# A mixture of experts on one core: gathered rows instead of one-hot products, weight tiles of 8 KB rows, four accumulators open at once

## The chip, the core and the metric

The kernel runs on one of the eight cores of a Trainium2 chip. The core has TensorE (PE in the profile, with its weight loads shown apart as PEld), VectorE (DVE), ScalarE (ACT), GpSimd (POOL) and SyncE (SP), which here only issues transfers; 16 DMA engines move data between DRAM and the on-chip memory SBUF, and PE writes into the accumulator memory PSUM. The metric is the time of one execution in microseconds of the device, the median of several runs.

## What is computed

Three model blocks follow each other on 512 tokens of 1024 features. The first two (an mLSTM and attention block, then a recurrent and gating block) and the mixers of the third are not touched. The third block ends in a mixture of 32 experts, four for each token, and a gated embedding. The reference, cut to that part and written in short:

```
logits = x @ router_w + router_b                     # [512, 32]
top4, idx = top_k(logits, 4);  gates = softmax(top4)
for expert e, for each token that chose e:
    h        = x_tok @ w_gate_up[e] + b_gate_up[e]   # [1024] @ [1024, 2048]
    gate, up = min(h[:1024], 7), clip(h[1024:], -7, 7)
    act      = (up + 1) * gate * sigmoid(1.702 * gate)
    y_tok   += gates[tok, e] * (act @ w_down[e] + b_down[e])
z = layer_norm(alpha * x + y);  out = layer_norm(alpha * z + sigmoid(z @ ple_gate_w + b) * (p @ ple_proj))
```

Each expert has 2 x 4 MB of gate and up weights and 4 MB of down weights, all float32.

## The kernel before

**Two-part products.** A float32 product is made of three passes in the format float32r: each operand is split into a high part and a low remainder (`hi`, `lo`), and `mm3` issues high by high, low by high and high by low (lines 165 to 167). A block of weights of 1 MB lands in a tile `wl` by a transfer that SP issues (line 92); ACT writes its high part `wh` (line 97) and DVE the remainder `wo` (line 98). `ring` hands out the tiles: in the experts' stage five `wl`, three `wh`, three `wo`.

**Routing.** `deepnorm` normalises token tile by token tile and calls `Moe.route`, which writes the rows to DRAM (`x3d`), chooses the experts, and leaves in `pos1` each token's slot in its experts (line 1454); it also splits x into the two parts `xs` (lines 109 and 110). An expert's first 96 tokens (`CAP`) are handled here; `crowded` takes any further ones in a branch after the end. Experts go in groups of three (`GRP`).

**Picking.** `mark` writes `hot`, which is 1 where a token has a slot (line 1507), for a group. `picked` multiplies x by it: four products of 128 x 288 over the four token tiles (line 1516) give 128 features of the slots of three experts, and one copy (line 1517 or 1550) keeps them. A group takes 64 such products. Those of the next group are spread over the experts of this one. `places` (four small products, line 1495) reads token number, gate and destination row of each slot.

**An expert.** `up` runs once for each half of the hidden columns: for the gate columns and then for the up columns it adds the bias by a product over 64 rows (line 1617: rows of the two parts of all experts' biases, picked by the column `sel` of the expert), and adds two weight blocks of 512 x 512 taken as four feature tiles. So one accumulator `pgu` is finished before the next is begun. `glu` reads them (lines 1535 to 1539), `turn` transposes the result (line 1525) and splits it into `h`. `down` takes four blocks of 512 x 512 for two accumulators `pd`, ACT scales them by the gate into `y` (line 1639), and POOL adds the rows to `yd` in DRAM by an indirect transfer (line 1722). In program order an expert is: first half of up, down of the expert before, second half of up; the compiler's scheduler interleaves the instructions of neighbouring calls on each engine, and each engine then runs its list in order.

**Accumulators.** PSUM's eight banks are shared as four `gemm` (for `pgu` and `pd`), three `aux` and one `hold`.

**The end.** `ple` reads `yd` back, normalises, and makes the last products; its gate biases are products over 64 rows too (line 1795).

Of the kernel before, what the change touches and what calls it, by code (L numbers as in the profile page):

```python
# [11 lines left out]
F32 = mybir.dt.float32  # L12
# [7 lines left out]
P = 128  # L20
S = 512
D = 1024
# [9 lines left out]
class Env:  # L32
    BANKS = {"gemm": 4, "aux": 3, "hold": 1}

    def __init__(self, ctx, tc):
        self.tc, self.nc = tc, tc.nc
        nc = self.nc
        self.cst = ctx.enter_context(tc.tile_pool(name="cst", bufs=1))
# [3 lines left out]
        self.psp = ctx.enter_context(tc.tile_pool(name="ps", bufs=4, space=bass.MemoryType.PSUM))  # L42
# [5 lines left out]
        self.n = 0  # L48
# [30 lines left out]

    def ps(self, s, tag="aux"):  # L80
# [19 lines left out]

    def wblock(self, w, k0, nk, c0, n, *more, **opts):
# [3 lines left out]
    def split(self, hi, lo, src, scale=None):  # L105
        """src * scale into two float32r parts."""
# [8 lines left out]
    def bank(self, ctx, n):  # L115
        """n tiles [128, 4, 512] on the right until ctx closes."""
# [20 lines left out]
    def give(self, *tiles):  # L137
        """What was read for the last time."""
# [6 lines left out]
    def lend(self, n):  # L145
        """n more tiles each for the two parts of weights; returns what ends that."""
# [12 lines left out]
    def acts(self, k, bank=None):  # L159
        """Tiles for a feature-major operand of k feature tiles: k/4 pairs [128, 4, 512]."""  # L160
# [8 lines left out]
    def gemm_tok(self, xs, K, w, c0, cn, consume, eng=None):  # L169
        """Token-major: consume(tt, col, n, psum) for psum[tok, col:col+n] = x @ w[:, col:col+n]."""  # L170
# [52 lines left out]
    def bcast(self, pool, src, n, tag):  # L223
        """A row of n values in DRAM onto all partitions."""
# [4 lines left out]
    def transpose_in(self, xs, t, src, k=KT):  # L229
        """src [tok of tile t, k*128 features] into the feature-major pairs xs."""  # L230
# [8 lines left out]
    def rstd(self, pool, ssq, n, eps, tag):  # L239
        """(ssq / n + eps) ** -0.5 of a few columns."""  # L240
# [8 lines left out]
    def rms(self, pool, x, gain, eps, out, scratch=None):  # L249
        """out = x * rsqrt(mean(x^2) + eps) * gain of one token tile [128, 1024]."""  # L250
# [6 lines left out]
    def layer_norm(self, pool, x, eps, out, gain, bias, tag=""):  # L257
        """out = (x - mean) * rstd * gain + bias of one token tile [128, 1024]."""
# [17 lines left out]
def block1(e, a, res, more):  # L276
    """The first block's x, and what the second's first product takes."""
# [17 lines left out]
    with ExitStack() as ph:  # L295
# [8 lines left out]
        # -------- i_k, i_w, m_i, m_f in one stationary block  # L304
# [33 lines left out]
        # index keys: norm over the 64 features, on both partition halves  # L338
# [24 lines left out]
        # relative bias: strips of 256 keys per head, less the value of far keys  # L363
# [23 lines left out]
        # causal mask inside one tile of 128 keys: 0 where key <= query  # L387
# [11 lines left out]
        # -------- mLSTM gates, a head per partition  # L399
# [37 lines left out]
        # selectors of a head's row: pairs of 64 partitions, and all 128  # L437
# [9 lines left out]
        # token-major columns of c, the key weights and the floor of the denominator  # L447
# [11 lines left out]
        # 0 where key <= query within one chunk of 64, keys on partitions  # L459
# [1408 lines left out]
```

## Time and profile before

| what | value |
|---|---|
| time, median of 3 runs | 3298.0 us (3294.18 to 3298.59) |
| profiled execution, first to last instruction | 3294.7 us |
| busy share of that span | PE 98%, PEld 74%, DVE 65%, ACT 47%, POOL 8% |
| DMA over the span | 626.96 MB, mean 190 GB/s |
| experts' stage, first bias product to last scatter | 1939.35 to 3208.18 us |

A busy share is an average over stages with different limits. What an edit in the experts' stage is worth has to be read from that stage alone, which is 39% of the span. PE's records overlap (a product's modelled end lies after the start of the next), so the spacing of the starts is what tells its pace.

### The profile page before, as it was taken

How to read it: one execution, taken by the hardware profiler on the slowest of the kernel's cores; microseconds unless marked ns; L12 is line 12 of the kernel's file. 1: busy time of each engine (PE TensorE's matmuls, PEld its weight loads, DVE VectorE, ACT ScalarE, POOL GpSimd, SP SyncE). 2: the span in 40 equal slices, each digit the busy share in tenths (PEclk: the TensorE clock that was granted, in tenths of full speed). 3: DMA queues.
4: the chain of work that ended last, by engine and by line, in shares of the span. 5: the costliest groups of instructions: out<-in, count | busy, mean ns of one | idle time of the engine just before them, and what ended most of it. 6: DMA issues, size and time to landing. Idle time of an engine off the chain costs nothing. (4 is left out here: it accounts for less than half of the span.)

```text
span 3294.7 us, 37481 instructions
## 1 busy us (share of the span) xinstructions
PE 3222.8 (98%) x15051; PEld 2434.6 (74%) x15051; DVE 2128.5 (65%) x2381; ACT 1564.5 (47%) x1655; POOL 272.7 (8%) x203
## 2 busy tenths in 40 slices
PE   7999999999999999999999999999999999999997
PEld 6776877878777788788778776666666666666665
DVE  5854687444636523822335778788888788888786
ACT  5343333323625223222322347777677667766662
POOL 2310011101000000200000100000000000000001
PEclk9997999999999999999999999999999999999999
DMA  4211465333222333232232259999999999999992
GB/s 143 77 39 62 147 218 201 115 109 97 64 64 64 89 113 122 87 109 92 83 119 90 91 204 330 332 324 319 330 329 329 327 327 325 323 331 325 328 328 104
DMA packets 324081, 626.96 MB, mean 190 GB/s; under 512 B 25144, under 2 KB 32672, under 8 KB 323834
## 3 DMA queue, kind: packets, MB, share of 16 engines
q1 hardware_dynamic: 320314, 611.89, 54.2%
q0 software_dynamic: 3584, 12.58, 1.9%
q8 instruction: 120, 1.97, 0.2%
q14 instruction: 63, 0.52, 0.0%
HBM read 603.43 MB, written 21.01 MB: 190 GB/s over the span
## 5 line engine op out<-in xcount | busy, mean ns | idle before, releaser
L98 DVE TENSOR_TENSOR wo<-wl,wh 128x2048 fp32r<-128x2048 f32 (+2 forms) x531 | 1190.3, 2254 | 627.8 <-ACT wh L97 625.8
L97 ACT ACTIVATE wh<-wl 128x2048 fp32r<-128x2048 f32 (+2 forms) x537 | 1009.0, 1885 | 744.6 <-PE pf L167 319.1
L165 PE MATMUL pf<-ah,wh 128*128 128x512 f32 (+1 forms) x1520 | 563.4, 371 | 0.6 <-ACT wh L97 0.6
L166 PE MATMUL pf<-ah,wo 128*128 128x512 f32 (+1 forms) x1520 | 562.2, 370 | 1.2 <-DVE wo L98 1.2
L167 PE MATMUL pf<-al,wh 128*128 128x512 f32 (+1 forms) x1520 | 561.5, 370 | 0.0
L165 PEld LDWEIGHTS pf<-ah,wh 128*128 128x128 f32 x1520 | 287.4, 189 | 56.4 <-ACT cy L727 6.9
L166 PEld LDWEIGHTS pf<-ah,wo 128*128 128x128 f32 x1520 | 287.0, 189 | 51.4 <-DVE wo L98 1.4
L167 PEld LDWEIGHTS pf<-al,wh 128*128 128x128 f32 x1520 | 286.5, 189 | 51.7 <-issue 3.7
L165 PE MATMUL pgu<-wh,xe 128*96 128x512 f32 x784 | 316.7, 404 | 0.0
L167 PE MATMUL pgu<-wo,xe 128*96 128x512 f32 x784 | 310.1, 396 | 1.8 <-DVE wo L98 1.7
L166 PE MATMUL pgu<-wh,xe 128*96 128x512 f32 x784 | 310.3, 396 | 0.0
L166 PE MATMUL pd<-wh,h 128*96 128x512 f32 x512 | 201.9, 394 | 0.0
L165 PE MATMUL pd<-wh,h 128*96 128x512 f32 x512 | 201.9, 394 | 0.0
L167 PE MATMUL pd<-wo,h 128*96 128x512 f32 x512 | 201.5, 393 | 0.1
L1722 POOL DMA_INDIRECT yd<-y,dst x32 | 79.1, 2472 | 1212.1 <-ACT y L1639 1112.1
L165 PEld LDWEIGHTS pgu<-wh,xe 128*96 128x96 f32 x784 | 126.3, 161 | 69.3 <-issue 22.2
L167 PEld LDWEIGHTS pgu<-wo,xe 128*96 128x96 f32 x784 | 126.6, 161 | 57.6 <-DVE wo L98 6.0
L166 PEld LDWEIGHTS pgu<-wh,xe 128*96 128x96 f32 x784 | 126.7, 162 | 45.9
L165 PE MATMUL pa<-wh,ah 128*128 128x512 f32 x352 | 143.0, 406 | 0.0
L167 PE MATMUL pa<-wo,ah 128*128 128x512 f32 x352 | 141.5, 402 | 0.2 <-DVE wo L98 0.2
L166 PE MATMUL pa<-wh,al 128*128 128x512 f32 x352 | 141.7, 402 | 0.0
L165 PE MATMUL pdn<-wh,ah 128*128 128x512 f32 x352 | 139.1, 396 | 0.7 <-ACT wh L97 0.7
(484 smaller groups left out, 4615.2 us busy)
## 6 DMA issues: line engine op xcount, KB each, us to landing
wl<-w_gate_up SPq DMA_DIRECT2D x256, 1024.0 KB
wl<-w_down SPq DMA_DIRECT2D x138, 1024.0 KB
wl<-w_in SPq DMA_DIRECT2D x54, 1024.0 KB
wl<-w_ada SPq DMA_DIRECT2D x24, 1024.0 KB
wl<-w_up SPq DMA_DIRECT2D x20, 1024.0 KB
wl<-w_ffn_in SPq DMA_DIRECT2D x20, 1024.0 KB
wl<-w_out SPq DMA_DIRECT2D x12, 1024.0 KB
wl<-w_ffn_out SPq DMA_DIRECT2D x10, 1024.0 KB
```

Source lines behind the costliest of these rows:

```text
L97: nc.scalar.activation(hi[:, :nk, :n], land[:, :nk, :n], AF.Copy)
L98: (eng or nc.vector).tensor_tensor(lo[:, :nk, :n], land[:, :nk, :n], hi[:, :nk, :n].bitcast(F32), op=ALU.subtract)
L165: mm(out, st[0], mv[0], start=first, stop=False)
L166: mm(out, st[1], mv[0], start=False, stop=False)
L167: mm(out, st[0], mv[1], start=False, stop=last)
L1722: self.e.nc.gpsimd.indirect_dma_start(out=self.yd, out_offset=bass.IndirectOffsetOnAxis(ap=dst[:, :1], axis=0), in_=y, in_offset=None, com ...
```

## The change

- The rows of an expert's tokens are gathered from `x3d` by an indirect transfer on POOL into `xg`, and transposed and split by `turn`, the helper that `h` goes through; `picked`, `share` and the split of x into `xs` are gone. In place of `xs`, `wh` and `wo` get two more tiles each (`lend`), so they have five.
- Weights come in through `wtile`: each transfer is 128 rows of 8 KB (a feature tile of all 2048 gate and up columns, or two neighbouring rows of `w_down` per partition) instead of 512 rows of 2 KB. `turn` gets `step=2` for `h`, which takes every second column, to suit the pairs of rows.
- `up` runs once for an expert, with its four accumulators open: all four biases first, then feature tile by feature tile. `glu` follows for both halves. `down` takes its two accumulators from `hold`; PSUM is laid out anew as four `gemm`, two `aux` and two `hold`.
- The bias products take all 128 rows (`sel` is 0 in the rows that don't belong), here and in `ple`.
- In an expert's program order the gather of the expert after next, and the two transposes of the next one's rows, stand between the feature tiles of `up`.

```diff
+    def wtile(self, src, **opts):
+        return self.weights(lambda land: [(land.rearrange("p a b -> p (a b)"), src)], 4, 512, **opts)
...
-    def picked(self, hot, f, part, out, copy, tag):
-        pt = e.ps("pt", tag)[:, :GRP * CAP]
-        for t in range(NT):
-            x = self.xs[part][t // 2].rearrange("p (h a) n -> p h (a n)", h=2)[:, t % 2, f * P:(f + 1) * P]
-            nc.tensor.matmul(pt, x, hot[:, t].rearrange("p e s -> p (e s)"), start=t == 0, stop=t == NT - 1)
-        copy(out, pt)
...
         for j in range(4):
-            nc.tensor.transpose(pt[:, j, :], src[:, j * P:(j + 1) * P], e.ident[:w, :w])
+            c = j // step * step * P
+            nc.tensor.transpose(pt[:, j, :], src[:, c:c + step * P].rearrange("p (f i) -> p i f", i=step)[:, j % step, :],
+                                e.ident[:w, :w])
...
+        e.layout(gemm=4, aux=2, hold=2)
+        back = e.lend(2)
...
+        def fetch(i):
+            pi, *took[i] = self.places(hots[p][:, :, j, :], self.tge[:, :, i, :])
+            src = wp.tile([P, 1], I32, tag="src", name=e.name("src"))[:CAP, :]
+            nc.vector.tensor_copy(src, pi[:, 0:1])
+            rows[i] = mp.tile([P, D], F32, tag="xg", name=e.name("xg"))[:CAP, :]
+            nc.gpsimd.indirect_dma_start(out=rows[i], out_offset=None, in_=self.xd,
+                                         in_offset=bass.IndirectOffsetOnAxis(ap=src[:, :1], axis=0))
...
+            if i < N_EXP:
+                side = {2: lambda: fetch(i + 2), 4: lambda: turn_x(i + 1, 0), 6: lambda: turn_x(i + 1, 1)}
+                gs = self.up(i, [xs.pop((i, g)) for g in range(2)], side)
             if i:
+                self.down(i - 1, hs, *took.pop(i - 1))
+            if i < N_EXP:
+                hs = [self.turn(g, entry("h", 2), 1.0 / SW, 2) for g in gs]
...
-    def up(self, i, xs, f):
+    def up(self, i, xs, side):
-        for c in (f * 512, D + f * 512):
-            p = e.ps("pgu", "gemm")[:CAP, :]
-            nc.tensor.matmul(p, self.sel[:2 * N_EXP, i:i + 1].to_broadcast([2 * N_EXP, CAP]), self.bgu[:2 * N_EXP, c:c + 512],
+        acc = [e.ps("pgu", "gemm")[:CAP, :] for _ in range(4)]
+        for c in range(4):
+            nc.tensor.matmul(acc[c], self.sel[:, i:i + 1].to_broadcast([P, CAP]), self.bgu[:, c * 512:(c + 1) * 512],
                              start=True, stop=False)
+        for k in range(KT):
+            hi, lo = e.wtile(w[k * P:(k + 1) * P, :], hold=self.pos1[:, 0, NT - 1:] if i == 0 and k > 1 else None)
+            for c in (0, 2, 1, 3):
+                e.mm3(acc[c], (xh[:, k % 4, :], xl[:, k % 4, :]), (hi[:, c, :], lo[:, c, :]), False, k == KT - 1)
+        return [self.glu(acc[f], acc[2 + f]) for f in range(2)]
...
-        acc = [e.ps("pd", "gemm")[:CAP, :] for _ in range(2)]
+        acc = [e.ps("pd", "hold")[:CAP, :] for _ in range(2)]
+        for j in range(4):
+            hi, lo = e.wtile(w[j * 256:(j + 1) * 256, :].rearrange("(p i) n -> p (i n)", i=2))
```

The scheduler's lists show three places where the change moves instructions. First DVE, in the middle of the stage, where it reads an expert's accumulators. Before, from one expert (`pgu` is an accumulator, `wo` a remainder of weights, L98 the split, L1535 to L1539 `glu`, L113 the split of `h`):

```order
L98 TENSOR_TENSOR wo_17463<-wl_17460,wh_17462 128x2048
L1538 TENSOR_SCALAR u_17455<-pgu_17414 96x512
L1539 SCALAR_TENSOR_TENSOR g_17452<-u_17455,g_17452 96x512
L98 TENSOR_TENSOR wo_17481<-wl_17478,wh_17480 128x2048
L98 TENSOR_TENSOR wo_17501<-wl_17498,wh_17500 128x2048
L1535 TENSOR_SCALAR g_17534<-pgu_17458 96x512
L113 SCALAR_TENSOR_TENSOR h_17540<-pt_17541,h_17540 128x384
L98 TENSOR_TENSOR wo_17519<-wl_17516,wh_17518 128x2048
```

Now, at the end of one expert's `up` (L103 is the split, L122 the split of `h`):

```order
L103 TENSOR_TENSOR wo_14197<-wl_14194,wh_14196 128x2048
L1535 TENSOR_SCALAR g_14212<-pgu_14027 96x512
L1538 TENSOR_SCALAR u_14215<-pgu_14029 96x512
L1535 TENSOR_SCALAR g_14218<-pgu_14028 96x512
L1539 SCALAR_TENSOR_TENSOR g_14212<-u_14215,g_14212 96x512
L1538 TENSOR_SCALAR u_14221<-pgu_14030 96x512
L103 TENSOR_TENSOR wo_14347<-wl_14344,wh_14346 128x2048
L1539 SCALAR_TENSOR_TENSOR g_14218<-u_14221,g_14218 96x512
L103 TENSOR_TENSOR wo_14365<-wl_14362,wh_14364 128x2048
L122 SCALAR_TENSOR_TENSOR h_14302<-pt_14303,h_14302 128x384
```

The reads of the four accumulators, which stood one or two at a time between splits of weights, now stand together, with a split among them.

Second, PE between the end of an `up` and the transposes of its result. Before, the rows just ahead of such transposes (L165 to L167 are `mm3`, L1525 the transposes of `turn`, `g_15424` the result of `glu`); fourteen products of `down`, of which three stand here, have been issued since the last of the accumulator that `g_15424` waits for:

```order
L167 MATMUL pd_15439<-wo_15444,h_15216 96x512
L165 MATMUL pd_15440<-wh_15461,h_15216 96x512
L166 MATMUL pd_15440<-wh_15461,h_15216 96x512
L1525 MATMUL pt_15517<-ident,g_15424 128x96 x4
L1516 MATMUL pt_15524<-spot,xs_12602 128x288 x2
L1516 MATMUL pt_15524<-spot,xs_12603 128x288 x2
```

Now (L174 to L176 are `mm3`, L1605 the bias, L1524 the transposes; `g_14790` and `g_14796` are the results of the `up` that has just ended with `pgu_14610`):

```order
L175 MATMUL pgu_14610<-wh_14774,xe_14475 96x512
L176 MATMUL pgu_14610<-wo_14775,xe_14475 96x512
L174 MATMUL pd_14803<-wh_14807,h_14591 96x512
L175 MATMUL pd_14803<-wh_14807,h_14591 96x512
L174 MATMUL pd_14804<-wh_14807,h_14591 96x512
L175 MATMUL pd_14804<-wh_14807,h_14591 96x512
L1605 MATMUL pgu_14896<-bgu,sel 96x512
L1605 MATMUL pgu_14897<-bgu,sel 96x512
L1605 MATMUL pgu_14898<-bgu,sel 96x512
L1605 MATMUL pgu_14899<-bgu,sel 96x512
L1524 MATMUL pt_14881<-ident,g_14790 128x96 x4
L1524 MATMUL pt_14889<-ident,g_14796 128x96 x4
```

Only four products of `down` and four biases stand between the end of `up` and the transposes of its result. Over the 32 experts the place of the first transpose repeats with a period of five: behind 8, 10, 48, 17 and 10 products.

Third, PE at the start of the stage. Before (L1436 is the last token tile's routing, L1452 and L1453 the counts for `pos1`, L1516 the picks, `hot` the marks):

```order
L1516 MATMUL pt_13146<-hot_13142,xs_12600 128x288
L1436 MATMUL pl_13089<-rw,xt_13076 128x32 x8
L1452 MATMUL pp_13109<-mask,ones 128x32 x3
L1516 MATMUL pt_13146<-hot_13142,xs_12600 128x288
L1516 MATMUL pt_13146<-hot_13142,xs_12601 128x288
L1516 MATMUL pt_13152<-hot_13142,xs_12602 128x288 x2
L1516 MATMUL pt_13152<-hot_13142,xs_12603 128x288
L1516 MATMUL pt_13158<-hot_13142,xs_12600 128x288 x2
L1516 MATMUL pt_13158<-hot_13142,xs_12601 128x288
L1516 MATMUL pt_13164<-hot_13142,xs_12602 128x288 x2
L1516 MATMUL pt_13164<-hot_13142,xs_12603 128x288
L1453 MATMUL pp_13109<-mask,upper 128x32
```

Now (L1501 is `places`, L1733 and L1740 are `biased`, L1488 `routed`, L1524 the transposes of gathered rows `xg`):

```order
L1501 MATMUL pi_13142<-tge,hot_13140 96x4 x3
L1733 MATMUL pg_13157<-ident,four_13158 128x128
L1501 MATMUL pi_13142<-tge,hot_13140 96x4
L1740 MATMUL pb_13164<-bgu,gs_13161 128x512 x2
L1740 MATMUL pb_13168<-bgu,gs_13161 128x512 x2
L1733 MATMUL pg_13173<-ident,four_13174 128x128
L1740 MATMUL pb_13180<-bgu,gs_13177 128x512 x2
L1740 MATMUL pb_13184<-bgu,gs_13177 128x512 x2
L1501 MATMUL pi_13189<-tge,hot_13140 96x4 x4
L1488 MATMUL pn_13204<-mask,ones 128x32 x4
L1524 MATMUL pt_13215<-ident,xg_13155 128x96 x4
```

The picks are gone from between the routing; the first expert now waits for a gather, and the work of `biased`, `places` and `routed`, which stood behind the first expert's products, stands ahead of them.

## Rows read from the trace of the kernel before

**Rows 1.** The page's parts 1 and 2: busy time, and 40 slices of the span.

```profile
PE 3222.8 (98%) x15051; PEld 2434.6 (74%) x15051; DVE 2128.5 (65%) x2381; ACT 1564.5 (47%) x1655; POOL 272.7 (8%) x203
...
PE   7999999999999999999999999999999999999997
```

**Rows 2.** Window of three experts: us, busy PE, PEld, DVE, ACT, POOL, clock, DMA, GB/s.

```profile
2512.62:2631.92 119.30, 118.93 (x546) 82.36 (x545) 97.82 (x71) 83.24 (x70) 7.63 (x4) 1.00 0.95 326
```

**Rows 3.** Waits from 2100 to 3200 us: total, times, longest, all in us.

```profile
ACT wh L97 <- PE pgu L166: 91.1, 91, 1.8
...
DVE g L1535 <- PE pgu L167: 68.6, 51, 2.1
DVE wo L98 <- ACT wh L97: 62.8, 100, 2.2
```

**Rows 4.** Timeline of PE around a bias: start us, duration us.

```profile
2519.29 0.39 PE L167 MATMUL pgu<-wo,xe 128*96 128x512 f32 x1
2519.61 0.47 PE L1617 MATMUL pgu<-bgu,sel 64*96 64x512 f32 x1
2520.01 0.48 PE L165 MATMUL pgu<-wh,xe 128*96 128x512 f32 x1
2520.33 0.39 PE L166 MATMUL pgu<-wh,xe 128*96 128x512 f32 x1
```

**Rows 5.** Timeline of PE where one accumulator group follows another.

```profile
2498.18 0.39 PE L167 MATMUL pgu<-wo,xe 128*96 128x512 f32 x1
2498.41 0.40 PE L165 MATMUL pd<-wh,h 128*96 128x512 f32 x1
```

**Rows 6.** Timeline of PE around transposes and picks.

```profile
2501.65 0.49 PE L1525 MATMUL pt<-ident,g 96*128 96x96 f32 x4
2501.93 0.77 PE L1516 MATMUL pt<-spot,xs 128*128 128x288 f32 x4
...
2510.95 1.75 PE L1516 MATMUL pt<-spot,xs 128*128 128x288 f32 x12
2512.62 0.47 PE L1617 MATMUL pgu<-bgu,sel 64*96 64x512 f32 x1
```

**Rows 7.** Line 1516 over the whole trace: ns min/median/max, first and last start.

```profile
L1516 PE MATMUL pt<-spot,xs x640: 289/294/404, 1962.1 to 3110.9; 128*128 128x288 f32 x160
```

**Rows 8.** Groups by form, 2512.62 to 2631.92 us: busy us, mean ns.

```profile
L98 DVE TENSOR_TENSOR wo<-wl,wh 128x2048 fp32r<-128x2048 f32 x37 | 83.9, 2285 | 7.1 <-ACT wh L97 7.0
...
L1535 DVE TENSOR_SCALAR g<-pgu 96x512 f32<-96x512 f32 x6 | 4.1, 687 | 8.2 <-PE pgu L167 8.2
...
L113 DVE SCALAR_TENSOR_TENSOR h<-pt,h 128x384 fp32r<-128x384 f32 x6 | 3.3, 547 | 0.0
...
L1507 DVE TENSOR_TENSOR spot<-slot,pos 128x1152 fp32r<-128x1152 f32 x1 | 1.3, 1345 | 0.0
```

**Rows 9.** DMA, 3172 to 3190 us: GB/s in 40 slices, then packets and total.

```profile
GB/s 373 400 387 378 391 369 410 396 382 405 396 382 401 400 378 391 396 382 387 391 291 382 419 387 405 423 246 118 414 391 414 410 391 260 191 332 246 410 419 319
DMA packets 3315, 6.60 MB, mean 367 GB/s; under 512 B 96, under 2 KB 96, under 8 KB 3314
```

**Rows 10.** DMA over 0 to 12 us, where 4 KB rows of x land: GB/s.

```profile
GB/s 0 0 0 0 0 0 137 177 328 328 314 396 287 259 259 232 273 314 287 314 423 382 423 437 437 396 423 437 410 437 383 195 106 171 188 91 42 22 8 17
```

**Rows 11.** DMA from 1706 to 1714 us, where the 8 KB rows of the biases land.

```profile
GB/s 0 0 0 0 0 0 0 0 0 0 0 0 0 0 0 0 0 0 0 0 0 0 205 246 205 205 205 246 0 123 287 369 266 287 0 328 369 184 266 174
```

**Rows 12.** DMA issues, 2512.62 to 2631.92 us: median us from issue to landing.

```profile
yd<-y,dst POOLq DMA_INDIRECT x4, 9.1
```

**Rows 13.** Timeline of PE and DVE at the start of the stage.

```profile
1919.27 1.97 PE L1432 MATMUL pt<-ident,xres 128*128 128x128 f32 x8 [4.33 <-DVE xres L269]
...
1926.47 0.36 DVE L1448 TENSOR_REDUCE mask<-hot 128x32 f32<-128x128 f32 x1
...
1929.51 0.22 DVE L1454 SCALAR_TENSOR_TENSOR pos<-pp,mask 128x32 f32<-128x32 f32 x1 [2.22 <-PE pp L1453]
...
1939.75 0.47 PE L165 MATMUL pgu<-wh,xe 128*96 128x512 f32 x1
```

More of the change, by code (lines that the diff above doesn't have):

```diff
@@ L1483, in routed @@
         nc.vector.tensor_copy(self.count[:, E:], most)
-    def share(self):
-        self.xs = [[self.e.slot("xs", F32R, 0) for _ in range(NT // 2)] for _ in range(2)]
     def places(self, hot, tge):
@@ L1547, in run @@
         e, nc, wp = self.e, self.e.nc, self.wp
-        groups = -(-N_EXP // GRP)
-        took, hots, parts = {}, {}, {}
-        copies = lambda o, i: nc.scalar.activation(o, i, AF.Copy), nc.vector.tensor_copy
-        def entry(nm):
-            return wp.tile([P, 2, 4, GRP * CAP], F32R, tag="xe", name=e.name(nm), bufs=3)
-        def mark(p, hot, *cuts):
-            hots[p] = hot
-            for t0, t1 in zip((0, *cuts), (*cuts, NT)):
-                self.chosen(hot[:, t0:t1], self.pos1[:, GRP * p:GRP * (p + 1), t0:t1])
@@ L1560, in pick @@
-        def pick(p, j, n, start=False):
-            every = [(g, k, part) for g in range(2) for k in range(4) for part in range(2)]
-            m = len(every)
-            for x, (g, k, part) in enumerate(every[j * m // n:(j + 1) * m // n]):
-                if not k and not part:
-                    both = self.spot[:, :8 * GRP * CAP].rearrange("p (a k n) -> p a k n", a=2, k=4) if g and p % 2 else entry("xe")
-                    for i in range(GRP):
-                        parts[GRP * p + i, g] = both, slice(i * CAP, (i + 1) * CAP)
-                both = parts[GRP * p, g][0]
-                self.picked(hots[p], 4 * g + k, part, both[:, part, k, :], copies[part if start else 0],
-                            ("hold", "gemm", "gemm", "gemm", "gemm")[x % 5] if start else "aux")
@@ new lines, in entry, with turn_x @@
+        def entry(nm, n):
+            return mp.tile([P, 2, 4, CAP], F32R, tag=nm, name=e.name(nm), bufs=n)
+        def turn_x(i, g):
+            if i < N_EXP:
+                xs[i, g] = self.turn(rows[i][:, g * 512:(g + 1) * 512], entry("xe", 3))
+        mark(0)
+        fetch(0)
+        self.biased(NT - 2)
+        self.biased(NT - 1)
+        fetch(1)
+        self.routed()
+        for g in range(2):
+            turn_x(0, g)
+        hs = None
+        for i in range(N_EXP + 1):
+            if i < N_EXP:
+                side = {2: lambda: fetch(i + 2), 4: lambda: turn_x(i + 1, 0), 6: lambda: turn_x(i + 1, 1)}
+                gs = self.up(i, [xs.pop((i, g)) for g in range(2)], side)
+            if i:
+                self.down(i - 1, hs, *took.pop(i - 1))
+            if i < N_EXP:
+                hs = [self.turn(g, entry("h", 2), 1.0 / SW, 2) for g in gs]
@@ L1618, in up @@
                              start=True, stop=False)
-            for k0 in (0, 4):
-                hi, lo = e.wblock(w, k0, 4, c, 512, hold=None if i or f or c == 0 and k0 == 0 else self.pos1[:, 0, NT - 1:])
-                xh, xl = xs[k0 // 4]
-                for k in range(4):
-                    e.mm3(p, (xh[:, k, :], xl[:, k, :]), (hi[:, k, :], lo[:, k, :]), False, k0 + k == 7)
-            acc.append(p)
-        return self.glu(*acc)
+        for k in range(KT):
+            hi, lo = e.wtile(w[k * P:(k + 1) * P, :], hold=self.pos1[:, 0, NT - 1:] if i == 0 and k > 1 else None)
+            xh, xl = xs[k // 4]
+            for c in (0, 2, 1, 3):
+                e.mm3(acc[c], (xh[:, k % 4, :], xl[:, k % 4, :]), (hi[:, c, :], lo[:, c, :]), False, k == KT - 1)
+            if k in side:
+                side[k]()
@@ L1807, in last @@
             nc.sync.dma_start(out[t * P:(t + 1) * P, :], zs[t])
-        first(0)
-        first(1)
-        for t in range(NT):
-            gate(t)
-            if t + 2 < NT:
-                first(t + 2)
-            if t:
-                last(t - 1)
-        last(NT - 1)
+        with e.tc.tile_pool(name=e.name("pl"), bufs=3) as lp:
+            first(0)
+            first(1)
+            for t in range(NT):
+                gate(t)
+                if t + 2 < NT:
+                    first(t + 2)
+                if t:
+                    last(t - 1)
+            last(NT - 1)
         e.give(own)
```

85 lines of the change are left out of this document (34 added, 51 removed).

## The prediction, made before the changed kernel ran

> **What bounds the kernel now.** I read the page first: PE is busy 98% of the span and in nearly every slice [rows 1], so the question is whether PE really paces the experts' stage, or only looks busy because its modelled ends overlap. The window of three experts decides [rows 2]: 119.30 us, so 39.77 us an expert, with PE busy 118.93 of them, DVE 97.82 (32.6 an expert), ACT 83.24, and the DMA engines 95% at 326 GB/s. Two resources are close to full, so I looked at who waits. ACT waits for PE to release `wh`, and DVE for PE's accumulators or for ACT [rows 3]; no wait of a compute engine on a transfer is among the long ones. So PE is the bound, the transfers arrive ahead of it, and their 95% is not a limit: when requests are queued, the same 2 KB rows run at 380 to 400 GB/s, and 367 in the mean of 18 us [rows 9]. What PE sheds is therefore gained, up to where DVE or DMA becomes the bound.
>
> **Part 1, the picks.** Products of 512 columns start 0.23 us apart [rows 4, 5]. Twelve picks take 2512.62 - 2510.95 = 1.67 us, 0.139 us each [rows 6]. 640 of them lie in the steady stage [rows 7] (64 more belong to the start): 640 x 0.139 = **-89 us**. Their copies are ACT's and cover nothing.
>
> **Part 2, the biases.** From the product ahead of a bias to the second behind it three steps take 2520.33 - 2519.29 = 1.04 us [rows 4], against 3 x 0.23 = 0.69 for products alone: 0.35 us lost at each product of 64 rows. A new accumulator isn't the cause, since `pd` begins 0.23 us behind `pgu` with products over 128 rows [rows 5]. With 128 rows I count a bias as any other product: 32 x 4 x 0.35 = **-45 us**; the eight in `ple`, of which part lies beside other waits, **-2**. Against this speaks a rule of the Trainium skill ("TensorE: Matmul & The Clock Gate", section "Why this matters for your kernels"): a product over 32 rows takes the same time as one over 128. By it the rows filled are no cost and this term would be 0, by the trace's rows it is 45. I take the rows, and keep 0 as a rival.
>
> **Part 3, the transposes.** Each expert adds eight transposes of gathered rows. Four of the same shape take 2501.93 - 2501.65 = 0.28 us [rows 6]; 31 experts x 8 x 0.07 = **+17 us** (the first expert's belong to the start). Those of `h` now read every second column; no row shows that. Below, nothing; above, each of 256 doubles: +18 us. I take 0, since the load of such a transpose is issued beside other products.
>
> **Part 4, the end of up.** Before, an accumulator was read while the next was being made. Now four end within ten products, and `glu` for both halves, six operations of 0.69 us on DVE [rows 8] with two on ACT between, stands at once ahead of the transposes. PE reaches the first transpose behind 8, 10, 48, 17 and 10 products in turn, that is 1.9, 2.3, 11, 3.9 and 2.3 us after the end of `up`. If DVE is free, the first accumulators are read before the last ends, and both halves are ready some 2.4 us after the end: a stall of at most 0.5 us in one case of five, 0.1 us an expert. If a split of 2.29 us [rows 8] has just begun, four operations more make the first half ready 5.3 us after the end: stalls of 3.4, 3.0, 0, 1.4 and 3.0 us, 2.2 an expert. What is queued behind on DVE are splits for later products, which five `wo` instead of three let run ahead; what is queued behind the transposes on PE is everything. I take 1.0 us, the middle, since the lists show a split in some of the groups: **+32 us**, with ends 3 and 70.
>
> **Part 5, DVE and ACT.** DVE's 32.6 us grow by two splits of gathered rows (0.55 each, by the split of `h`, [rows 8]) and one conversion of a column to some 33.9 us. The new period by parts 1 to 4 is 39.77 - 21.3 x 0.139 - 1.4 + 0.56 + 1.0 = **37.0 us**, so DVE is 92% busy: covered, but with 3 us to spare instead of 7. ACT loses 5.3 copies and gains two splits: no cost.
>
> **Part 6, the transfers.** An expert moves 12 x 1.0486 MB of weights, 0.39 MB of scatter and now 0.39 MB of gather, 13.37 MB. In 37.0 us that is 361 GB/s. Below: the rows of 4 KB at the kernel's start reach 423 to 437 GB/s [rows 10], so longer rows are no slower, and an expert needs 31 us. Above: the only rows of 8 KB, small loads that hardly fill the engines, show 205 to 369 GB/s [rows 11]. I take the large loads of 4 KB as nearest (1 MB each now, queued) and cost this at 0. The Trainium skill ("HBM Reference", section "Specifications (TRN2)") gives 358 GB/s per core: by it the period would be 37.3 us at least and the sum some 12 us more; the trace's 367 over 18 us [rows 9] does not agree.
>
> **Part 7, the gathers.** Each stands on POOL ahead of or behind a scatter and is used an expert later. A scatter takes 9.1 us to land [rows 12] and POOL is idle most of the time [rows 2]: hidden by some 35 us of products. Only the first is on the path. There the counts for `pos1` no longer wait behind picks: the mask is there at 1926.8, so `pos1` at about 1927.5 instead of 1929.5 [rows 13]; then marks (1.3 us, and 1.3 for the next group, [rows 8]), `places`, four small operations, together about another 1.4: the gather is issued at about 1931.5. It lands after 9.1 us at most, as the scatter, or half of that since it adds nothing, and transposes and split take 1 more: first weight product at 1937 to 1942, against 1939.75 [rows 13]. PE idles then, as it did before 1919.27 [rows 13], and may start at the lower clock (up to 2 us). In return `biased`, `places` and `routed`, which lay among the first expert's products, lie in this gap; I set the one against the other. Sum 0, ends -3 and +5.
>
> At the far end `down` of the last expert now waits for both halves of `h` (transpose, ACT, DVE): **+1 us**.
>
> **The sum.** -89 - 45 - 2 + 17 + 32 + 0 + 1 = -86 us. Against the profiled execution's span of 3294.7 us this is 3209; that execution stands 0.1% under the median of the runs, 3298.0, so on the runs' scale I forecast **3212 us**.
>
> **Rivals.**
> - *The end of up stalls in full* (part 4's upper end): 38 us more, 3250. For it: before, 14 products stood between, now often 8 or 10. Against: accumulators end one after the other, and DVE has more tiles ahead.
> - *The bias is no faster*: the 0.35 us belong to the product itself (its column of weights repeated 96 times, or the hop to another accumulator), not to its 64 rows; 45 us less gained, 3257. For it: nothing here shows such a product with 128 rows. Against: the hop alone costs nothing [rows 5].
> - *DVE becomes the bound*, the rival on the other side. DVE runs its list in order and now idles 39.77 - 32.6 = 7.2 us an expert. If that idling is of its order (it waits for an accumulator while a landed block lies behind), it stays, and a period is 33.9 + 7.2 = 41.1 us: 3298 + 32 x 1.3 = 3340. It decides from 5.9 us of idling up. Against: those waits are for PE, which was late, and shrink when DVE is the later one; two more `wo` let splits run ahead.
> - *The transfers become the bound.* If longer rows bring nothing over the 326 GB/s of the stage [rows 2], 13.37 MB take 41.0 us: 3337. Against: [rows 9, 10].
> - *The change does nothing for PE*: if all it sheds turns into waits for `wo`, the period stays at 39.77 and the time at 3298.
>
> **How the numbers follow.** Forecast 0.60; full stall 0.16; bias no faster 0.06; DVE 0.09; transfers 0.05; nothing 0.04. The best case, with a stall of 0.1 us an expert and 3 us gained at the start, is 3298 - 118 = 3180. From 3184 to 3262 the range holds the forecast's own ends and the two slower-but-gaining rivals; the case of doubled transposes of `h` (+18) fits inside. Faster by over 0.2% (about what a measurement of this kernel can tell from no change): 0.60 + 0.16 + 0.06 = 0.82, with a little of the last rival 0.84; same 0.03; slower 0.13.
>
> **What would show it.** Right: starts of products 0.23 us apart on both sides of a bias; eight transposes for x of 0.07 us each; an expert in about 37 us; PE's waits, now nil, at the transposes of `g` and about 1 us an expert; DVE over 90%; DMA near 360 GB/s at a lower share of the engines than 95%. Wrong: PE waiting for `wo` all through `up` (DVE), ACT waiting for transfers of `w_gate_up` (DMA), a step of 0.3 us or more still beside each bias, or a start of the first products later than 1945.

## The result, and the profile after

The changed kernel takes 3427.4 us (median of 4 runs, 3425.75 to 3432.0), the kernel before 3297.9 in the same job: 1.0397 times as long, 95% interval 1.0382 to 1.0412. The forecast was 3212. The profiled execution's span is 3423.9 us.

The page's head and slices, against [rows 1]: PE's share falls from 98% to 93% and the slices of the experts' stage (the last two fifths) are mostly no longer 9s. In part:

```profile
PE 3199.0 (93%) x14603; PEld 2406.7 (70%) x14603; DVE 2144.8 (63%) x2467; ACT 1515.4 (44%) x1547; POOL 295.0 (9%) x237
PE   7999999999999999999999899988998988989887
PEclk9997999999999999999999899999999999999998
DMA  4212474332112332322323588887888878888863
```

Busy time by window in the stage, first three experts' length, then all of its steady part; columns are the window, busy time of PE, PEld, DVE, ACT, POOL, the granted clock, the DMA share and GB/s. Against [rows 2]:

```profile
2512.00:2632.00 120.00, 101.33 (x437) 68.73 (x436) 88.08 (x74) 67.22 (x53) 9.83 (x6) 0.94 0.79 292
2100.00:3200.00 1100.00, 981.35 (x4225) 673.09 (x4223) 830.34 (x658) 662.07 (x503) 83.87 (x50) 0.94 0.83 306
```

PE, DVE and ACT are all less busy than before, the transfers too (83% at 306 GB/s, before 95% at 326). Nothing has become the bound; something makes all of them wait. The waits of 2100 to 3200 (engine, what waited, for what; total us, times, longest; rows of POOL, PEld and smaller ones left out), against [rows 3]:

```profile
DVE wo L103 <- ACT wh L102: 186.9, 89, 7.2
ACT wh L102 <- PE pgu L175: 110.8, 43, 7.8
ACT wh L102 <- DMA wl<-w_gate_up: 90.1, 36, 5.9
PE pgu L174 <- ACT wh L102: 62.2, 30, 7.0
ACT xe L118 <- PE pgu L176: 52.4, 10, 5.7
ACT wh L102 <- DMA wl<-w_down: 33.0, 11, 5.2
PE pd L176 <- DVE wo L103: 29.9, 15, 2.7
```

PE, which waited for next to nothing before (busy 118.93 of 119.30 us, [rows 2]), now waits for ACT's and DVE's parts; ACT waits for transfers and also for PE. It is a circle, and the chain of work that ended last goes through all of it. A piece of that chain (start, length, what; the first two rows are a load and its split; pieces left out are marked):

```profile
2350.95 4.78 DMA wl<-w_gate_up
2355.84 1.93 ACT wh L102
2357.79 2.30 DVE wo L103
...
2360.49 8.36 DMA wl<-w_gate_up
2368.94 1.92 ACT wh L102
2370.90 0.74 PE pgu L174
2371.64 0.43 PE pgu L175
...
2374.29 0.23 PE pgu L175
```

A load is issued at 2360.49, when a buffer has just been freed, and lands 8.4 us later; by the time that ACT has split it, PE has stood 5.7 us (the row that follows). Then PE's products come 0.43 us apart, and from 2374.3 on 0.23 again: the granted clock was near its lower level of 1.2 GHz at first (0.52, in the first of the two windows).

```profile
2370.90 0.74 PE L174 MATMUL pgu<-wh,xe 128*96 128x512 f32 x1 [5.67 <-ACT wh L102]
```

```profile
2370.90:2374.20 3.30, 3.30 (x8) 1.96 (x9) 2.27 (x1) 0.00 (x0) 0.00 (x0) 0.52 1.05 415
2374.30:2376.30 2.00, 2.00 (x10) 1.37 (x9) 0.29 (x1) 0.80 (x2) 0.00 (x0) 1.00 0.73 262
```

Why was that load so late? The program itself says so. These are SP's loads at this place, in the order in which SP issues them, two left out; the number behind a name's last underscore grows in the order of the program's text, and nearly in that of use:

```
L97 DMA wl_2562_16151<-w_gate_up_3 128x2048
...
L97 DMA wl_2567_16177<-w_gate_up_3 128x2048
L97 DMA wl_2570_16195<-w_gate_up_3 128x2048
...
L97 DMA wl_2588_16272<-w_down_3 128x2048
L97 DMA wl_2591_16290<-w_down_3 128x2048
L97 DMA wl_2559_16133<-w_gate_up_3 128x2048
```

The load of 2360.49 is `wl_2559`, issued behind five tiles (2562, 2567, 2570, 2588, 2591) that are used after it. In the whole stage a load stands 2.0 places from its place in the order of use on average; in the kernel before, nearly every one stands in its own. ACT's and DVE's splits are out of order too (1.6 and 1.5 places from the order of the text). Nothing at run time does this: the order of each engine's instructions is fixed when the program is built.

An expert now takes 43.7 us (steps from one expert's first bias to the next repeat in fives, some 218 us), against 39.77 before and 37.0 forecast.

### The profile page after: what moved, and what is told of

It reads as the page before. It is cut to its first block, busy times and chain, and to the rows that moved or that the text cites. A ratio compares the mean times of both kernels' runs of the same rounds, so it can differ in the third digit from the quotient of the medians.

```text
span 3423.9 us, 36601 instructions
## 1 busy us (share of the span) xinstructions
PE 3199.0 (93%) x14603; PEld 2406.7 (70%) x14603; DVE 2144.8 (63%) x2467; ACT 1515.4 (44%) x1547; POOL 295.0 (9%) x237
## 5 line engine op out<-in xcount | busy, mean ns | idle before, releaser
L103 DVE TENSOR_TENSOR wo<-wl,wh 128x2048 fp32r<-128x2048 f32 (+2 forms) x531 | 1189.0, 2259 | 771.2 <-ACT wh L102 760.5
L174 PE MATMUL pf<-ah,wh 128*128 128x512 f32 (+1 forms) x1520 | 561.6, 370 | 0.6 <-ACT wh L102 0.6
L176 PE MATMUL pf<-al,wh 128*128 128x512 f32 (+1 forms) x1520 | 560.0, 369 | 0.0
L174 PE MATMUL pgu<-wh,xe 128*96 128x512 f32 x1024 | 428.0, 418 | 75.7 <-ACT wh L102 75.2
L175 PE MATMUL pgu<-wh,xe 128*96 128x512 f32 x1024 | 423.6, 414 | 0.0
L176 PE MATMUL pgu<-wo,xe 128*96 128x512 f32 x1024 | 388.3, 414 | 12.9 <-DVE wo L103 12.7
L174 PEld LDWEIGHTS pf<-ah,wh 128*128 128x128 f32 x1520 | 286.8, 189 | 58.5 <-ACT cy L736 6.9
L176 PEld LDWEIGHTS pf<-al,wh 128*128 128x128 f32 x1520 | 286.1, 188 | 50.6 <-issue 3.7
L174 PEld LDWEIGHTS pgu<-wh,xe 128*96 128x96 f32 x1024 | 174.6, 171 | 162.7 <-ACT wh L102 90.5
L176 PEld LDWEIGHTS pgu<-wo,xe 128*96 128x96 f32 x1024 | 169.6, 171 | 102.5 <-DVE wo L103 34.5
L176 PE MATMUL pd<-wo,h 128*96 128x512 f32 x512 | 201.9, 409 | 38.7 <-DVE wo L103 37.9
L175 PEld LDWEIGHTS pgu<-wh,xe 128*96 128x96 f32 x1024 | 175.4, 171 | 72.2 <-issue 0.9
L174 PE MATMUL pd<-wh,h 128*96 128x512 f32 x512 | 207.5, 405 | 3.4 <-ACT wh L102 3.4
L175 PE MATMUL pd<-wh,h 128*96 128x512 f32 x512 | 205.1, 401 | 0.0
L1713 POOL DMA_INDIRECT yd<-y,dst x32 | 68.9, 2152 | 976.3 <-ACT y L1630 651.1
L176 PEld LDWEIGHTS pd<-wo,h 128*96 128x96 f32 x512 | 85.4, 167 | 84.2 <-DVE wo L103 48.5
L174 PE MATMUL pa<-wh,ah 128*128 128x512 f32 x352 | 141.9, 403 | 0.0
L176 PE MATMUL pa<-wo,ah 128*128 128x512 f32 x352 | 140.5, 400 | 0.2 <-DVE wo L103 0.2
```

Source lines behind the costliest of these rows:

```text
L103: (eng or nc.vector).tensor_tensor(lo[:, :nk, :n], land[:, :nk, :n], hi[:, :nk, :n].bitcast(F32), op=ALU.subtract)
L174: mm(out, st[0], mv[0], start=first, stop=False)
L175: mm(out, st[1], mv[0], start=False, stop=False)
L176: mm(out, st[0], mv[1], start=False, stop=last)
L1713: self.e.nc.gpsimd.indirect_dma_start(out=self.yd, out_offset=bass.IndirectOffsetOnAxis(ap=dst[:, :1], axis=0), in_=y, in_offset=None, com ...
```

## Experiments

Each time is a median, the ratio is to the kernel before on the same chip (95% interval). "An expert" is the mean distance of first bias products.

**Theories at the start.** A: loads and splits out of order. B: the 8 KB rows. C: four accumulators that end together. D: gathered rows that come late.

**1. The loads in order.**

```diff
         for dst, src in srcs(land):
-            nc.sync.dma_start(dst, src)
+            ins = nc.sync.dma_start(dst, src)
+            if keep:              # the loads of wtile alone
+                self.behind(ins)  # issue order only: behind the load before
```

> The changed kernel with one edit: the loads of the experts' weights are issued on SP in the order in which the program's text writes them, each behind the one before; the work on ScalarE and VectorE then follows in that order too. Sizes, rows, buffers and accumulators stay. Theory A (the order): the 117 us of TensorE's waits in 25 experts, and the low granted clock behind them, come from tiles that were loaded and split ahead of an earlier one. Then the time falls from 3427 to between 3200 and 3265 us, an expert takes 37 to 39 us instead of 43.7, and the granted clock of the stage is back at 0.98 or more. Theory B (8 KB rows, or the transfers as such): the order matters little, ScalarE goes on waiting for w_gate_up; 3380 to 3430 us. Theory C (four accumulators that end together leave TensorE without work at the end of every up): 1.5 to 2.5 us an expert stay, 3260 to 3300 us.

Measured 3431.8 us, 1.0408 [1.0394, 1.0422]: no gain, though every load and every split now stands in the text's order and ACT hardly waits for a transfer any more. Theory A as I had put it falls: that order is not enough. What the disorder costs by itself run 1 can't say, since tying the loads also gave PE, ACT and DVE other lists. ACT's long waits are now for PE and DVE (`h` for `pd` 124.0 us in 25 experts, `g` for DVE 116.6, `xe` for `pgu` 98.4): it stands in its list at something that isn't there yet.

**2. Without the lent tiles.** The lines `back = e.lend(2)` and `back()` are gone, so `wh` and `wo` have three tiles as before the change.

> The changed kernel without the two more tiles each that are lent to the two parts of the weights: three of each again, as before the change, while the landing tiles stay five. The order of the loads is then the program's once the first two experts are past, though not at the start of the stage. Theory A (the order): 3200 to 3290 us, with ScalarE waiting more for products that read the parts, since a part is free later. Theory B (8 KB rows): 3400 us or more, fewer buffers making it no better. If the lent tiles are needed and the order is not the cause: slower than 3427.

Measured 3293.1 us, 0.9985 [0.9976, 0.9994], just above what theory A gave: 134 us come back by taking buffers away. The kernel also shows two paces in itself. Four experts early, and four later, in the same kernel with the same rows, buffers and accumulators:

```profile
2032.25:2176.58 144.33, 144.33 (x674) 103.09 (x674) 133.33 (x107) 106.66 (x81) 21.94 (x8) 1.00 0.96 353
2608.84:2768.96 160.12, 152.34 (x674) 105.45 (x673) 133.93 (x107) 104.84 (x81) 28.95 (x8) 0.97 0.90 335
```

36.1 us an expert and PE busy throughout, then 40.0. Between the two stands another order of instructions: early, PE has 16 products of `down` between the end of `up` and the first transposes of `h`; later it has 4; and DVE has five or six splits of weights between the second split of `h` and the first of x, later four. At the end of an `up` of the second kind:

```profile
2607.43 0.69 DVE L1535 TENSOR_SCALAR g<-pgu 96x512 f32<-96x512 f32 x1 [0.82 <-PE pgu L176]
2607.92 0.39 PE L174 MATMUL pd<-wh,h 128*96 128x512 f32 x1
...
2609.83 0.68 DVE L1538 TENSOR_SCALAR u<-pgu 96x512 f32<-96x512 f32 x1
2610.43 2.28 DVE L103 TENSOR_TENSOR wo<-wl,wh 128x2048 fp32r<-128x2048 f32 x1
2612.76 0.47 PE L176 MATMUL pd<-wo,h 128*96 128x512 f32 x1 [1.73 <-DVE wo L103]
```

The remainder `wo` that PE needs next is made by DVE only from 2610.4 on, behind five operations of the glu (the first and the last are shown), and DVE had idled 0.82 us for the first of them with that split behind it. So theory E: it is the order, on all engines and not on SP alone.

**3 and 4. The two terms by themselves.** Run 3 is the kernel before with 128 rows for the biases:

```diff
-self.sel[:2 * N_EXP, i:i + 1].to_broadcast([2 * N_EXP, CAP]), self.bgu[:2 * N_EXP, c:c + 512],
+self.sel[:, i:i + 1].to_broadcast([P, CAP]), self.bgu[:, c:c + 512],
```

(and the same in the last gate.) Run 4 is the changed kernel with `up`, `down`, the 2 KB blocks, three tiles for each part, PSUM's layout and the 64-row biases of the kernel before, so that only the picks are replaced.

> The kernel before with the bias products alone made 128 rows deep (the selecting matrix with zero rows below, in the experts and in the last gate). My prediction's term: 0.35 us less for each of 128 products, -45 us and -2 us: 3251 us, PE with no idle time round the bias rows. By the rival that a 64-row product costs no more than another: 3298 us, no change.

> The x rows gathered and transposed in place of the picks, and nothing else: up in two halves of two accumulators, weights as 2 KB rows in blocks of four, three tiles for each part, 64-row bias products. My prediction's terms: -89 us for the picks, +17 us for the transposes: 3226 us. Theory D (the gathered rows are late, since the gather takes 9.8 us to land and waits for the place products): TensorE waits for xg at the transposes, 3260 to 3300 us. The place of the products that pick rows between two halves of up also gave ScalarE and VectorE time; if that time was needed, the saving is smaller, and the rows of wo on VectorE say so.

Run 3: 3258.3 us, 0.9876 [0.9861, 0.9892]; an expert in 38.4 us. Run 4: 3221.5 us, 0.9762 [0.9747, 0.9777]; an expert in 37.2 us, PE without a wait. Both terms are there: 38.5 and 75.3 us. Theory D falls.

**5. Both terms together**, still in two halves.

> The gathered and transposed rows together with the 128-row bias products; up in two halves of two accumulators, weights as 2 KB rows in blocks of four, three tiles for each part. If the two terms add: 3221 less 38.5 us, 3183 us, an expert in 36.0 us with TensorE busy throughout. If the transfers bound it (the gathered rows alone already moved 357 to 362 GB/s in an expert of 37.25 us, and 36.0 us need 3.5% more): 3205 to 3221 us with ScalarE waiting for w_gate_up.

Measured 3185.3 us, 0.9654 [0.9636, 0.9673]: the terms add (111.8 us, against 38.5 + 75.3 = 113.8), an expert takes 36.1 us, and this is the fastest kernel of the study.

```profile
2200.00:2400.00 200.00, 199.93 (x927) 140.09 (x926) 182.40 (x145) 147.55 (x112) 30.83 (x12) 1.00 1.04 368
```

**6. Shorter rows.** Run 2 with each load cut in four.

```diff
-        return self.weights(lambda land: [(land.rearrange("p a b -> p (a b)"), src)], 4, 512, **opts)
+        cut = src.shape[1] // 4
+        return self.weights(lambda land: [(land[:, c, :], src[:, c * cut:(c + 1) * cut]) for c in range(4)], 4, 512, **opts)
```

> The changed kernel without the lent tiles, each load of 128 rows cut into four loads of 2 KB pieces; tiles, products and their order stay. Theory B (8 KB rows are the cost that is left): towards 3190 us. Theory C and theory E (the four accumulators that end together, or the order of the instructions): 3285 to 3300 us as with 8 KB rows, the expert in 40.4 us and TensorE waiting 1.7 us for wo at the second block of down.

Measured 3297.1 us, 1.0001 [0.9992, 1.0011], against 3293.1 with 8 KB rows. Theory B falls.

**7 and 8. PE's order held**, without and with the lent tiles. Each PE instruction of the stage is tied to be issued behind the one before it in the text, and the text is written in the order of run 2's fast experts; run 8 holds SP's loads too. The edit, shortened:

```diff
+        row = [x for x in instructions_of_the_stage if x.engine == PE]
+        for x, y in zip(row, row[1:]):
+            e.tc.add_manual_dep(y, x.name, ...)      # issue order only
```

> The changed kernel without the lent tiles, TensorE's instructions in the stage held to one order for every expert: 96 products of up with the transposes of x behind the fifth and seventh block, 15 products of the down before, the transposes of the first half of h, the four bias products of the next expert, the other 33 products of down, the transposes of the second half. Theory E (the order decides; the experts 3 to 7 of the kernel without lent tiles ran in such an order in 36.07 us and the others, transposes of h after 4 products of down, in 40.4): 36.1 us for every expert, 3170 to 3200 us. Theory C (four accumulators that end together): 3270 to 3295 us, the wait of TensorE for wo only in another place. Theory B (8 KB rows): 3290 us.

> The changed kernel with all its buffers, the lent ones too, with the loads on SP and the instructions on TensorE both held to one order (the one of the run without lent tiles; the first experiment held the loads alone). Theory E (the order decides, buffers do no harm): 3165 to 3200 us. Theory L (the lent tiles do the harm themselves: six slots shared by landing tiles and both parts, so that a landing tile waits for a slot that a part holds): 3290 to 3430 us, SP waiting on wo and landing tiles late.

Run 7: 3230.1 us, 0.98 [0.9781, 0.982], 37.05 us an expert. Run 8: 3430.0 us, 1.0394 [1.0377, 1.0412]. Run 7 lies between what theories E and C gave. So PE's order gives 63 us where no tiles are lent (ACT's and DVE's lists have the same pattern in runs 2 and 7), and nothing where they are: theory E, with PE and SP alone, fails in run 8. Either the tiles do harm by themselves (L), or the lists of ACT and DVE, still free, differ. They do differ. ACT's list at the end of one `up`, in run 8 (`wh_3199` is the first tile of the `down` that follows, `xe` the split of x, `g` the activation of the glu):

```
L112 ACTIVATE wh_3189_19119<-wl_3188_19117 128x2048
L128 ACTIVATE xe_3186_19109<-pt_3187_19110 128x384
L1546 ACTIVATE g_3191_19135<-g_3191_19135 96x512
L112 ACTIVATE wh_3199_19152<-wl_3198_19150 128x2048
L1546 ACTIVATE g_3193_19141<-g_3193_19141 96x512
```

and with the list of run 7, where the names come out the same (run 11, below):

```
L112 ACTIVATE wh_3189_19119<-wl_3188_19117 128x2048
L112 ACTIVATE wh_3199_19152<-wl_3198_19150 128x2048
L128 ACTIVATE xe_3186_19109<-pt_3187_19110 128x384
L112 ACTIVATE wh_3202_19170<-wl_3201_19168 128x2048
L1546 ACTIVATE g_3191_19135<-g_3191_19135 96x512
```

In run 8 the split of `wh_3199` stands two places further back. DVE's list moves in the same way: its split `wo_3200` stands behind five operations of the glu in run 8, and ahead of all six in run 11. The trace of run 8 at an earlier expert, whose split stands in the same place of ACT's list, shows what that does (rows left out between these):

```profile
2612.44 0.49 PE L1534 MATMUL pt<-ident,xg 96*128 96x96 f32 x4
2612.97 0.49 ACT L128 ACTIVATE xe<-pt 128x384 fp32r<-128x384 f32 x1 [3.59 <-PE pt L1534]
2614.68 0.63 ACT L1546 ACTIVATE g<-g 96x512 f32<-96x512 f32 x1 [1.22 <-DVE g L1545]
2615.22 1.90 ACT L112 ACTIVATE wh<-wl 128x2048 fp32r<-128x2048 f32 x1
2617.14 2.29 DVE L113 TENSOR_TENSOR wo<-wl,wh 128x2048 fp32r<-128x2048 f32 x1
2617.16 0.48 PE L184 MATMUL pd<-wh,h 128*96 128x512 f32 x1 [1.50 <-ACT wh L112]
```

ACT idles 3.59 us for PE's transposes and 1.22 for the glu, with the split that PE needs next behind both; then PE waits for it. PE makes ACT wait, ACT makes PE wait, and neither is busy. Over the stage of run 8, PE waits 120.8 us for `wo` and 15.2 for `wh`; some half of the wait for `wo` (61.8 us) ends with a split that DVE began as soon as ACT's `wh` was there, the rest with one that stood behind DVE's other work. So both lists have a part.

**9 and 10. Fewer landing tiles.** Without the lent tiles the loads may use more of the bank's six slots, so landing tiles were a rival cause (M). Four slots are taken out of use in run 7 and in run 5.

```diff
+        held = [e.slot("held", F32, 0) for _ in range(4)]
+        for t in held:
+            nc.gpsimd.memset(t[:, 0, 0:1], 0.0)
         ...
+        for t in held:                       # after the last expert's gate is known
+            nc.gpsimd.tensor_copy(t[:CAP, 0, 0:1], self.end)
```

> The run with TensorE's order held (no lent tiles, three for each part, 3230 us) with four of the six slots of the bank, from which two classes of landing tiles are drawn, taken out of use for the whole stage; the order of the instructions on every engine stays what it was, bar a few at the stage's start. So at most five landing tiles are in use at once, as in the kernel before and in the changed one; in the run with all six slots up to seven were (loads issued at 2634.5 and 2635.0 us while the five tiles ahead of them were still read). Theory M (landing tiles: what the lent tiles cost is that the bank's slots no longer take loads that run ahead): 41 to 44 us an expert, 3360 to 3440 us, with ScalarE waiting for the transfers of w_gate_up. Theory P (the lent tiles harm by the order in which splits and transposes are then issued on ScalarE and VectorE, which the scheduler makes from what it believes of the buffers, and not by landing tiles): 37.1 to 38 us an expert, 3230 to 3265 us.

> The fastest version so far (gathered rows, 128-row biases, two halves, 3185 us) with four of the bank's six slots taken out of use in the same way: five landing tiles at most. Theory M: with five landing tiles a load comes 5 tiles ahead at most; the kernel before lived with that at 39.8 us an expert (a landing tile used for 16 us, 3.2 us a tile), and 36.1 us need 15.0 us for each; so 37.5 to 39.5 us an expert, 3230 to 3300 us. Theory P: 36.1 to 36.5 us an expert, 3185 to 3200 us.

Run 9: 3231.0 us, 0.9799 [0.9783, 0.9815], against 3230.1. Run 10: 3190.4 us, 0.9668 [0.9652, 0.9685], against 3185.3, with the same 36.1 us an expert. Theory M falls: five landing tiles are enough in a good order.

**11 and 12. All lists held, with the lent tiles.** In run 11 ACT's and DVE's instructions, from the third expert on, get a place in units of a tile (a split 1.5 tiles ahead of its products, `xe`, `glu`, `h` and `y` at theirs) and are tied in that order, so that PE, ACT and DVE have the pattern of run 7's lists in the steady part, and SP the text's. Theory P says that the lists of ACT and DVE are the cause, theory Q that it is something in the lent tiles themselves. Run 12 moves every split one tile earlier, which three tiles for each part don't allow.

```diff
+            with self.key(12 * i + k - 1.5):       # run 12: - 2.5
                 hi, lo = e.wtile(w[k * P:(k + 1) * P, :], ...)
```

> The changed kernel with all its buffers (five tiles for each part, four of the ten from the bank), with TensorE, ScalarE, VectorE and SP in the stage each held to the order of the run that had no lent tiles and TensorE's order (3230 us, 37.05 us an expert). Theory P (the lent tiles cost only through the order on ScalarE and VectorE: there a tile's split stood behind the split of x or behind the activation of the glu that it stood ahead of in the run without them): 37.0 to 37.3 us an expert, 3225 to 3240 us. Theory Q (something in the lent tiles themselves, such as where they lie or the slots they share with landing tiles): 42 to 44 us an expert, 3400 to 3430 us.

> The same, with every split of a tile on ScalarE and VectorE placed one tile earlier against the products (three ahead in place of two), which needs the lent tiles. If the 1 us that TensorE waits for wo at the end of each up in the run without lent tiles is the late split (theory P): 36.1 to 36.4 us an expert, 3190 to 3210 us. If the five landing tiles bound what can be split ahead: 37 to 40 us an expert, 3230 to 3320 us, with ScalarE waiting for the transfers. Theory Q: 3400 us or more.

Run 11: 3220.5 us, 0.9763 [0.9747, 0.978], 37.0 us an expert. Run 12: 3207.1 us, 0.9717 [0.9701, 0.9733], 36.1 us. The windows of run 11 and then run 12:

```profile
2512.00:2632.00 120.00, 117.20 (x542) 82.90 (x541) 108.26 (x89) 86.55 (x67) 22.97 (x6) 1.00 0.98 360
```

```profile
2512.00:2632.00 120.00, 120.00 (x559) 85.77 (x558) 111.54 (x90) 88.51 (x69) 26.05 (x6) 1.00 1.00 378
```

Theory P holds and Q falls: run 11 has the tiles, slots and transfers of run 8 and the same lists on PE, SP and POOL; the lists on ACT and DVE are others, and it takes 210 us less, a little less even than P gave. Theory C falls with run 12: four accumulators that end together, and PE without a wait at 36.1 us an expert, as with two halves. Which of the two lists does more was not separated by a run, and why the lists came out this way with lent tiles was not looked into.

## Why the prediction was wrong

**The step that failed** is in part 4: "What is queued behind on DVE are splits for later products, which five `wo` instead of three let run ahead", and again among the rivals, "two more `wo` let splits run ahead". More tiles were taken to mean more lead, so that a stall was costed at the transposes alone (0.1 to 2.2 us an expert, taken as 1.0) and none for a split that comes late. In its place the runs show that an engine's lead is set by its list: ACT does nothing behind an instruction that waits, and with the lent tiles the splits stand late in the lists at the ends of `up`. PE's waits and the lower clock behind them come to some 7 us an expert (below). The changed kernel against the same kernel with the lists of run 11 is 3427.4 - 3220.5 = 207 us; on the way there, leaving out the lent tiles alone gives 134 (run 2), PE's order then 63 more (run 7), and with the tiles lent and PE's order held, the lists of ACT and DVE decide over 210 us (runs 8 and 11).

The lists of the changed kernel had it. In the group of PE's list that stands ahead of the prediction, the four products of `down` behind the end of `up` use `wh_14807` alone. Its remainder, which `down` needs next, stands on DVE's list behind six operations of the glu, and behind two remainders that are used later. The trace at that place:

```profile
2170.55 1.29 PE L1524 MATMUL pt<-ident,g 96*128 96x96 f32 x8 [0.22 <-DVE g L1539]
2170.92 4.48 DVE L103 TENSOR_TENSOR wo<-wl,wh 128x2048 fp32r<-128x2048 f32 x2
2173.26 0.74 PE L176 MATMUL pd<-wo,h 128*96 128x512 f32 x1 [1.42 <-DVE wo L103]
```

PE waits 0.22 us at the transposes, where the stall was costed, and 1.42 for `wo` behind them. The lists of PE and DVE were read ahead of the prediction for the reads of the accumulators, not for the place of each split, and none of ACT or SP stands there.

The Trainium skill ("TensorE: Matmul & The Clock Gate", section "Architectural detail: the array is 16× 32×32, not 1× 128×128") calls the queues of ScalarE and VectorE strictly first in, first out; run 8's rows agree, with 3.59 us of waiting in front of a split.

**How the 43.7 us come about.** The forecast's 37.0 holds 36.0 of work and 1.0 of stall. PE's waits in the window of 2100 to 3200 sum to some 116 us over 25 experts, 4.6 an expert (PE's two rows among the waits above, 14.2 at the transposes of gathered rows and 9.6 for `wo` in `up`). That gives 40.6. Of the other 3.1, the lower clock after waits accounts for about 2.6 by my estimate: it was granted at 0.94 in that window, 1.00 in [rows 2], and 6% of 43.7 is 2.6. The last 0.5 is not accounted for.

**Part by part**, as the runs have it:
- *Picks and transposes of x* (-89 + 17 = -72): run 4 has -75.3. Right.
- *Biases* (-45 and -2): run 3 has -38.5. An expert is 1.3 us shorter, 0.33 a product against 0.35; the stage also begins later there, first bias at 1945.4 against 1939.35. Right but for that. The Trainium skill ("TensorE: Matmul & The Clock Gate", section "Why this matters for your kernels") gives a single product over 32 rows the time of one over 128, by which the term would have been 0; in this stream of products run 3 does not agree.
- *End of up* (+1.0 an expert): wrong, as above. That run 11 takes 37.0 us, 0.9 more than run 5 in two halves, is luck: it has other lists than those that I costed, and its 0.9 are late splits (run 12 takes 36.1), not a stall at the transposes.
- *Transposes of `h` with a step* (0): the load takes 211 ns instead of 140 and the transpose 281 instead of 251 (208 and 273 in run 12, at the full clock), yet run 12 has 36.1 us an expert with PE never idle, as run 5 without the step. Right.
- *DVE* (92%, covered): 93% in run 12, and PE has no wait for it there; 90% in run 11, where PE waits some 0.7 us an expert for `wo` in `down`. In the changed kernel DVE is 75% busy and PE waits for it all the same: the share was right for a good order and said nothing of the wait.
- *Transfers* (0): 360 GB/s in run 11, 378 in run 12, and run 6 shows 2 KB and 8 KB rows alike. Right. The sign that was named against it, ACT waiting for `w_gate_up`, did come (90.1 us), but run 1 takes it away and the time stays.
- *Start* (0): the first weight product comes at 1936.1 in the changed kernel, forecast 1937 to 1942. The number is near, by luck in part: `pos1` was there at 1921.1 and the gather issued at 1925.9, some 6 us ahead of the forecast, and the time until 1934.6, when the transposes begin, goes to the gather and to the work of `biased`, `places` and `routed`. A gather lands in 9.8 us (median of 25 in the stage), as a scatter does (10.4), not in half of that.

With the lists of run 11 the sum, 3212, is 0.3% off, but the forecast was for the lists that it had before it. The rival on the other side ("DVE runs its list in order", 3340) had the mechanism, but for DVE alone and as a leftover of 7 us of idling; it missed that the lists themselves would change. The range (to 3262) left out what it should have held: that a change of buffers rewrites four lists.

## What to carry to other kernels

- Where a scheduler orders the instructions, a change of buffers can rewrite every engine's list (two more tiles for each part: 134 us, run 2). Before costing anything, look in the lists for the place of each split: one that PE needs next and that stands behind an instruction that waits is a stall that no busy share shows. Loads out of order are a sign of it; putting them right alone gained nothing (run 1).
- Here all engines were less busy at once, each waiting for another, because their lists blocked each other, and more buffers did not mend that. Hold the lists (run 11 and 12), or keep the form whose lists are good (run 5).
- Try the parts of a large change alone: two of these were worth 112 us, and hidden behind 240 us of the rest.

## What the runs showed of the hardware

- A DMA share near 1 is no limit by itself: 95% of the engines' time moved 326 GB/s before [rows 2], 96% moved 353 early in run 2, and 104% moved 368 in run 5. The Trainium skill ("HBM Reference", section "Specifications (TRN2)") gives 358 GB/s as one core's share and some 425 for a core that streams alone; the last of these windows went past the first, and none up to the second.
- A product over 64 rows among products over 128 costs 0.33 us more than one over 128 (run 3 against the kernel before).
- After a wait of 5.7 us the granted clock was 0.52 over the next 3.3 us, then 1.00.
